# Two tiles by one DMA in the merge stage of a streaming encoder step

## The chip, the cores and the metric

One core of one Trainium2 chip runs the whole program. The metric is device time in microseconds of one execution; three executions of the kernel before were timed, and one more was taken with the hardware profiler. All tensors are float32. Matrix products are done as three products of split operands (high x high, high x low, low x high), which is why many tiles have an "h" and an "l" part.

## The reference

One layer for 2048 new frames and 64 frames of a running stream, model width 1024:

```python
def layer_inputs(x, norm_g, w_in, b_gate, qn_g, kn_g):
    h = rmsnorm(x, norm_g) @ w_in                     # 1024 -> 6144 columns
    qa, ka, va, za, qb, kb, vb, zb, ga, gb = jnp.split(h, _split_points(), axis=-1)
    ...
    ga = jax.nn.sigmoid(ga + b_gate[0])               # merge gates, 1024 wide each
    gb = jax.nn.sigmoid(gb + b_gate[1])

def layer_output(x, oa, ob, za, zb, ga, gb, subln_g, lam_init, w_oa, w_ob, w_out):
    oa = (rmsnorm(oa, subln_g) * (1.0 - lam_init)).reshape(B, T, W_A) * jax.nn.silu(za)
    ob = rmsnorm(ob).reshape(B, T, W_B) * jax.nn.silu(zb)
    m = ga * (oa @ w_oa) + gb * (ob @ w_ob)
    return x + m @ w_out
```

oa is the output of differential attention, ob that of multi-scale retention, each 512 wide; attention and retention themselves are not touched by the change.

## The kernel before

The program has three parts that overlap. The input projection (line L554 of the matmuls) makes q, k, v, the gate inputs za and zb and the merge-gate inputs ga and gb, and stores them to DRAM, transposed (channel on the partition, frame along the row). Attention and retention read q, k, v back and store their branch outputs to DRAM as oaT and obT. Then comes the merge, and after it the output projection with the residual.

The merge works on 8 column groups g of GW = 264 frames. For each group and each branch br (0 is attention, 1 is retention), four row tiles kt of 128 channels are loaded: the branch output `on` and its gate's input `z`. `og_fin` does z = silu(z) on ScalarE, on = on x z on POOL, a cast to the high part ogh on ScalarE, and the difference, the low part ogl, on VectorE. For each group there are eight output tiles ct. `m_tile` does 12 matmuls per branch into one PSUM bank (mm for branch 0, s for branch 1): 24 matmuls per tile (L1722, L1723, L1724). The two merge gates gt of the tile are loaded by `gates`, put through tanh on ScalarE by `gate`, multiplied with the two PSUM results on VectorE (L1742), added on POOL (L1746), and stored as mT by `m_fin`. Only then can that gate buffer be loaded again.

The branch weights w_o_diff and w_o_ret are loaded by `load_wo` in pieces of 128x256 (wst) and split into high and low parts (woh and wol, woq). They share the buffers "oz" with on and z. Beside the merge, `b_prep` loads the output weights w_out and splits them and sums of them (bh and bl, bht and blt; L1815, L1818). The output stage `y_group` (L1934) multiplies mT, loaded as a and split as ah and al, with those. VectorE and POOL prepare sums of a (L1756, L1758), and u holds partial results of the output.

ogh and ogl have three sets of four pairs of buffers: two under the tag "og" and one under "ob". One set is in use by each branch of the current group, so the four pairs for branch 1 of the next group find room only when branch 0 of the present group's last tile is done.

What sets the order: the kernel is written out by a list scheduler of its own. Generators (`spawn`, `loop`) advance by priority on a model of the engines' times: `take` waits until a buffer of a tag is free by the model, `give` says from when it is, `ld` and `st` issue DMAs, and P, A, V and G advance the model's TensorE, ScalarE, VectorE and POOL. On the chip each engine then works through its own list in order, and every wait is a real semaphore. All DMAs of the program, loads (L135) and stores (L140), are issued by one queue, SP, in order.

Of the kernel before, what the change touches and what calls it, by code (L numbers as in the profile page):

```python
# [8 lines left out]
F32 = mybir.dt.float32  # L9
# [17 lines left out]
GW = 264  # L27
# [5 lines left out]
BUFS = {"thi": 1, "tlo": 2, "ev": 3, "q": 2, "K": 4, "V": 4, "ath": 2, "atl": 2,  # L33
        "ws": 3, "w": 12, "r_o": 1, "r_sq": 1, "r_y": 1, "r_hi": 1, "r_lo": 1, "state": 2,
        "mm": 2, "s": 2, "at": 2, "pv": 1, "tp": 1,
        "oz": 11, "og": 16, "ob": 8, "gt": 10, "wa": 16, "st": 13, "ac": 16, "u": 9, "xt": 10}
LAT = 250.0
SLACK = 400.0
PACE = 700.0
# [20 lines left out]
class Hybrid:  # L60
# [1545 lines left out]
    def split_fin(self, tag, h, l, s, t, on_pool, slot, key):  # L1606
# [12 lines left out]
        self.give(tag, t)  # L1619
        slot[key] = t  # L1620

    def load_wo(self, br, q):
        csl = slice(256 * (q % 2), 256 * (q % 2) + 256)
        for kt in range(4):
            hl, slot = self.wo[br][kt]
            h, l = hl[q // 2]
            yield from self.take("oz")
            s = self.sb(self.z3p, [128, GW], "oz", "wst")[:, :256]
            t = self.ld(s, self.i[("w_o_diff", "w_o_ret")[br]][0, 128 * kt:128 * kt + 128, 256 * q:256 * q + 256],
                        1 << 17)  # L1630
            self.spawn(self.split_fin("oz", h[:, csl], l[:, csl], s, t, (kt + q) % 3 == 0, slot, q), 2)
            yield self.pe

    def out_prep(self):
        pa = self.z3p
        self.wo = [[([[self.sb(self.zq, [128, 512], "wa", "woq", F32R) for n in "hl"],
                      [pa.tile([128, 512], F32R, tag=f"wo{n}{br}{kt}", name=f"wo{n}{br}{kt}") for n in "hl"]], {})
                    for kt in range(4)] for br in range(2)]
        for br in range(2):
            yield from self.load_wo(br, 0)  # L1640
        for g in range(8):
            gsl = slice(GW * g, GW * g + GW)
            for br, (oT, zT) in enumerate(((self.oaT, self.zaT), (self.obT, self.zbT))):
                for kt in range(4):
                    yield from self.take("oz", 2)
                    on = self.sb(pa, [128, GW], "oz", "on")
                    z = self.sb(pa, [128, GW], "oz", "z")
                    self.ld(z, zT[kt][:, gsl], 1 << 17)
                    t = self.ld(on, oT[kt][:, gsl], 1 << 17)
                    og = []  # L1650
                    self.ogs.append(og)
                    self.spawn(self.og_fin(on, z, t, og, (2 * g + br) % 3 == 2), 1)
                    yield self.pe
            if g == 0:
                self.spawn(self.gates(), 0)
                for q in range(1, 4):
                    for br in range(2):
                        yield from self.load_wo(br, q)
                yield lambda: self.b_left < 13

    def og_fin(self, on, z, t, og, third):
        nc = self.nc
        yield t
        nc.scalar.activation(z, z, AF.Silu)
# [12 lines left out]
        nc.scalar.copy(h, on)  # L1677
        t = self.A(GW, t)
        yield t
        nc.vector.tensor_sub(l, on, h.bitcast(F32))  # L1680
        t = self.V(GW + 80, t)
        self.give("oz", t)
        og.append((h, l, t))

    def gates(self):
        for n in range(64):
            g, ct = divmod(n, 8)
            yield from self.take("gt", 2)
            pair = [self.sb(self.z3p, [128, GW], "gt") for _ in range(2)]
            for gt, gT in zip(pair, (self.gaT, self.gbT)):  # L1690
                t = self.ld(gt, gT[ct][:, GW * g:GW * g + GW], 1 << 17)
            self.spawn(self.gate(n, ct, pair, t), 0)
            yield self.pe

    def gate(self, n, ct, pair, t):
# [39 lines left out]
    def m_fin(self, g, ct, pss):  # L1735
        nc = self.nc
        yield lambda: 8 * g + ct in self.gts
        gs, tg = self.gts.pop(8 * g + ct)
        for br in range(2):
            ps, tag, t = pss[br]  # L1740
            yield max(t, tg)
            nc.vector.scalar_tensor_tensor(out=gs[br], in0=gs[br], scalar=1.0, in1=ps, op0=ALU.add, op1=ALU.mult)  # L1742
# [553 lines left out]
```

## Time and profile before

| | us |
|---|---|
| median of 3 runs | 1947.14 (1945.34 to 1948.15) |
| the profiled execution | 1945.82 |
| its span, first to last instruction | 1944.0 |
| TensorE busy | 1927.5 |
| VectorE, ScalarE, POOL busy | 1166.6, 964.9, 490.1 |
| merge, first to last matmul start | 1574.9 to 1772.9 |
| output stage from | 1773.0 |

In rows of the profile, PE is TensorE, DVE is VectorE, ACT is ScalarE and SPq is SP's queue; "out<-in" names the tiles an instruction writes and reads; what stands in brackets at the end of a timeline row is how long the engine stood idle before it, and the instruction that ended this. A timeline row "x4" merges four instructions. The mean granted clock of TensorE over the span is 0.998 of full speed.

### The profile page before, as it was taken

The numbers are of one execution on the slowest core, as the hardware profiler recorded it, in microseconds if no ns is written. First come the engines' busy times: TensorE is split into PE (matmuls) and PEld (weight loads), VectorE is DVE, ScalarE is ACT, GpSimd is POOL, SyncE is SP. The second block draws the span as 40 slices with busy tenths as digits, with TensorE's granted clock in tenths as the row PEclk, the third lists the DMA queues.
The fourth block names the chain that finished last, engine by engine and source line by source line (L and its number), as shares of the span: only waits on it lengthen the run. The fifth ranks groups of instructions, "written<-read, shape, count | busy, mean of one in ns | idle before, by whom it ended". The sixth has DMA issues, their size and how long they took to land.

```text
span 1944.0 us, 33842 instructions
## 1 busy us (share of the span) xinstructions
PE 1927.5 (99%) x11984; PEld 1731.2 (89%) x11984; DVE 1166.6 (60%) x2798; ACT 964.9 (50%) x2072; POOL 490.1 (25%) x429
## 2 busy tenths in 40 slices
PE   9999999999999999999999999999999999999999
PEld 8779999999988899999998888888888889998887
DVE  6753777646666336648856757845773376545643
ACT  7443766544434235535765646544563445653321
POOL 4310112112122121211121111112113356543422
PEclk9999999999999999999999999999999999999999
DMA  7747454335566655654344253363133678866651
GB/s 235 240 151 199 143 143 132 106 102 156 163 192 187 166 148 168 202 183 141 112 120 128 76 146 96 99 185 116 63 99 108 190 229 259 264 196 189 190 151 65
DMA packets 372074, 303.32 MB, mean 156 GB/s; under 512 B 77440, under 2 KB 334720, under 8 KB 371904
## 3 DMA queue, kind: packets, MB, share of 16 engines
q1 hardware_dynamic: 371904, 301.16, 52.6%
q8 instruction: 94, 1.54, 0.4%
q14 instruction: 76, 0.62, 0.1%
HBM read 195.87 MB, written 100.14 MB: 152 GB/s over the span
## 4 chain that ended last, share of the span: by engine, by line
PE 88%; DVE 5%; DMA 3%; POOL 1%; issue 1%; ACT 1%; SPq 1%; DVEq 0%; POOLq 0%; ACTq 0%
PE mm L554 51%; PE mm L1934 4%; PE s L1052 3%; PE s L1053 3%; PE at L1160 3%; PE at L1934 2%; PE pv L1139 2%; PE pv L1140 2%; PE pv L1138 2%; PE s L1934 1%; PE s L1723 1%; PE s L1724 1%; PE pv L1521 1%; PE mm L1723 1%; PE s L1722 1%
## 5 line engine op out<-in xcount | busy, mean ns | idle before, releaser
L514 POOL TENSOR_TENSOR wl<-ws,wh 128x512 fp32r<-128x512 f32 x191 | 261.4, 1380 | 896.2 <-ACT wh L504 544.9
L554 PE MATMUL mm<-xh,wh 128*128 128x512 f32 (+2 forms) x1280 | 460.7, 360 | 0.0
L554 PE MATMUL mm<-xh,wl 128*128 128x512 f32 (+2 forms) x1280 | 452.7, 354 | 0.0
L554 PE MATMUL mm<-xl,wh 128*128 128x512 f32 (+2 forms) x1280 | 451.9, 353 | 0.0
L554 PEld LDWEIGHTS mm<-xh,wl 128*128 128x128 f32 x1280 | 241.0, 188 | 31.7
L554 PEld LDWEIGHTS mm<-xh,wh 128*128 128x128 f32 x1280 | 241.4, 189 | 29.1 <-issue 0.2
L554 PEld LDWEIGHTS mm<-xl,wh 128*128 128x128 f32 x1280 | 241.6, 189 | 27.8
L554 PE MATMUL mm<-wh,xh 128*128 128x256 f32 (+1 forms) x768 | 236.7, 308 | 0.0
L554 PE MATMUL mm<-wh,xl 128*128 128x256 f32 (+1 forms) x768 | 231.3, 301 | 0.0
L554 PE MATMUL mm<-wl,xh 128*128 128x256 f32 (+1 forms) x768 | 231.0, 301 | 0.0
L1175 DVE TENSOR_TENSOR atl<-at,ath 128x512 fp32r<-128x512 f32 (+1 forms) x144 | 93.7, 659 | 136.2 <-ACT ath L1173 136.1
L504 ACT CAST wh<-ws 128x512 fp32r<-128x512 f32 x192 | 117.0, 617 | 112.6 <-PE mm L554 90.3
L1091 ACT ACTIVATE row<-row,a_mx 128x1024 f32<-128x1024 f32 (+7 forms) x160 | 153.7, 962 | 24.5 <-DVE a_mx L1071 24.3
L554 PEld LDWEIGHTS mm<-wh,xh 128*128 128x128 f32 x768 | 146.3, 190 | 7.1 <-issue 0.5
L554 PEld LDWEIGHTS mm<-wl,xh 128*128 128x128 f32 x768 | 146.4, 191 | 6.7 <-issue 0.5
L554 PEld LDWEIGHTS mm<-wh,xl 128*128 128x128 f32 x768 | 146.3, 190 | 5.5
L865 DVE TENSOR_TENSOR ev<-mm,rsb 128x512 f32<-128x512 f32 x140 | 83.0, 593 | 112.8 <-PE mm L554 112.4
L1173 ACT CAST ath<-at 128x512 fp32r<-128x512 f32 (+1 forms) x144 | 78.7, 563 | 141.5 <-PE at L1160 138.4
L1061 DVE CUSTOM_DVE_ANT_0 row<-s,dfar 128x512 f32<-128x512 f32 (+2 forms) x192 | 118.2, 630 | 46.4 <-PE s L1053 45.9
L1052 PE MATMUL s<-K,q 128*128 128x512 f32 (+3 forms) x320 | 118.4, 374 | 0.7 <-DVE a_acc L1061 0.7
L1053 PE MATMUL s<-K,q 128*128 128x512 f32 (+3 forms) x320 | 115.2, 362 | 0.0
L1110 ACT ACTIVATE row<-row,a_w 128x1024 f32<-128x1024 f32 (+4 forms) x96 | 85.1, 898 | 34.4 <-DVE a_w L1105 31.2
(342 smaller groups left out, 4193.5 us busy)
## 6 DMA issues: line engine op xcount, KB each, us to landing
ws<-in_w_in_dram SPq DMA_DIRECT2D x192, 256.0 KB, 3.1
q<-qT SPq DMA_DIRECT2D x128, 128.0 KB, 3.0
V<-vN SPq DMA_DIRECT2D x24, 512.0 KB, 5.4
K<-kT SPq DMA_DIRECT2D x48, 256.0 KB, 4.3
a<-mT SPq DMA_DIRECT2D x34, 256.0 KB, 4.1
gt<-gaT SPq DMA_DIRECT2D x64, 132.0 KB, 3.2
gt<-gbT SPq DMA_DIRECT2D x64, 132.0 KB, 3.1
mT<-gt SPq DMA_DIRECT2D x64, 132.0 KB, 3.0
```

The lines of the kernel that those rows point to most:

```text
L504: self.nc.scalar.copy(h, st)
L514: self.nc.gpsimd.tensor_sub(l, st, h.bitcast(F32))
L554: nc.tensor.matmul(ps, p, q, start=c == 0 and i == 0, stop=c == KC - 1 and i == 2)
L865: nc.vector.tensor_mul(ev, ps, rsb)
L1052: nc.tensor.matmul(ps, q1s, kk, start=True, stop=False)
L1053: nc.tensor.matmul(ps, q2s, kk, start=False, stop=True)
L1061: nc.vector.tensor_tensor_reduce(out=units[k0 // 1024][:, k0 % 1024:k0 % 1024 + n], in0=ps, in1=tab, scale=-SLOPES[h], scalar=3.0e38, op0= ...
L1091: nc.scalar.activation(u, u, AF.Exp, bias=mx, scale=-1.0, accum_out=lp[:, k:k + 1])
L1110: nc.scalar.activation(u1, u1, AF.Identity, scale=w[:, 1:2])
L1173: nc.scalar.copy(ah[:, :w], at[:, :w])
L1175: nc.vector.tensor_sub(al[:, :w], at[:, :w], ah[:, :w].bitcast(F32))
L1934: nc.tensor.matmul(q[b], u, v, start=fresh and c == 0 and m == 0, stop=c == 3 and m == 2, skip_group_check=True)
```

## The change

Each branch output and its gate's input get one DRAM tensor ozT with the two side by side for each partition, and the two merge gates one tensor gT. The stores write to views of them. One DMA then loads on and z as one tile of 128x2x264, one DMA loads both merge gates of a tile, and one DMA loads two pieces of a branch's weights. The buffers change from 11 single tiles to 5 double ones under "oz", and from 10 single to 5 double under "gt". Arithmetic instructions stay the same in number and size. A double buffer is given back once, when both halves are done: z's half no longer returns after POOL's product, and gt's second half no longer after POOL's sum.

```diff
-        "oz": 11, "og": 16, "ob": 8, "gt": 10, "wa": 16, ...
+        "oz": 5, "og": 16, "ob": 8, "gt": 5, "wa": 16, ...
 ...
-        self.zaT = tc.dram_tile([4, 128, 8 * GW], F32, name="zaT")
-        self.zbT = tc.dram_tile([4, 128, 8 * GW], F32, name="zbT")
-        self.gaT = tc.dram_tile([8, 128, 8 * GW], F32, name="gaT")
-        self.gbT = tc.dram_tile([8, 128, 8 * GW], F32, name="gbT")
-        self.oaT = tc.dram_tile([4, 128, 8 * GW], F32, name="oaT")
-        self.obT = tc.dram_tile([4, 128, 8 * GW], F32, name="obT")
+        self.ozT = [tc.dram_tile([4, 128, 2, 8 * GW], F32, name=f"ozT{br}") for br in range(2)]
+        self.gT = tc.dram_tile([8, 128, 2, 8 * GW], F32, name="gT")
 ...
     def load_wo(self, br, q):
-        for kt in range(4):
+        for k2 in range(2):
             yield from self.take("oz")
-            s = self.sb(self.z3p, [128, GW], "oz", "wst")[:, :256]
-            t = self.ld(s, self.i[("w_o_diff", "w_o_ret")[br]][0, 128 * kt:128 * kt + 128, 256 * q:256 * q + 256],
-                        1 << 17)
-            self.spawn(self.split_fin("oz", h[:, csl], l[:, csl], s, t, (kt + q) % 3 == 0, slot, q), 2)
+            s = self.sb(self.z3p, [128, 2, GW], "oz", "wst")[:, :, :256]
+            t = self.ld(s, self.i[("w_o_diff", "w_o_ret")[br]][0, 256 * k2:256 * k2 + 256, 256 * q:256 * q + 256]
+                        .rearrange("(c p) n -> p c n", p=128), 1 << 18)
+            box = []
+            for u in range(2):
+                kt = 2 * k2 + u
+                ...
+                self.spawn(self.split_fin("oz", h[:, csl], l[:, csl], s[:, u], t, (kt + q) % 3 == 0, slot, q, box), 2)
 ...
     def out_prep(self):
-                    yield from self.take("oz", 2)
-                    on = self.sb(pa, [128, GW], "oz", "on")
-                    z = self.sb(pa, [128, GW], "oz", "z")
-                    self.ld(z, zT[kt][:, gsl], 1 << 17)
-                    t = self.ld(on, oT[kt][:, gsl], 1 << 17)
+                    yield from self.take("oz")
+                    both = self.sb(pa, [128, 2, GW], "oz", "oz")
+                    t = self.ld(both, self.ozT[br][kt][:, :, gsl], 1 << 18)
 ...
     def og_fin(self, on, z, t, og, third):
         nc.gpsimd.tensor_mul(on, on, z)
         t = self.G(GW, t)
-        self.give("oz", t)
 ...
     def gates(self):
-            yield from self.take("gt", 2)
-            pair = [self.sb(self.z3p, [128, GW], "gt") for _ in range(2)]
-            for gt, gT in zip(pair, (self.gaT, self.gbT)):
-                t = self.ld(gt, gT[ct][:, GW * g:GW * g + GW], 1 << 17)
+            yield from self.take("gt")
+            both = self.sb(self.z3p, [128, 2, GW], "gt")
+            t = self.ld(both, self.gT[ct][:, :, GW * g:GW * g + GW], 1 << 18)
 ...
     def m_fin(self, g, ct, pss):
         nc.gpsimd.tensor_add(gs[0], gs[0], gs[1])
         t = self.G(GW, t)
-        self.give("gt", t)
```

SP issues 1408 DMAs in place of 1552. TensorE's list is the same instruction by instruction. The lists of ScalarE, VectorE and POOL hold the same instructions and are the same up to the merge's first loads; from there on the scheduler puts them in another order.

ScalarE at the passage from column group 1 to group 2, the splits for branch 1 of group 2 (ogh) being the last in each list shown. Before:

```order
L1664 ACTIVATE z<-z 128x264
L1698 ACTIVATE gt<-gt,bg 128x264 x2
L1664 ACTIVATE z<-z 128x264
L1815 CAST bht_18301<-wst 128x512
L1815 CAST bht_18299<-wst 128x512
L1698 ACTIVATE gt<-gt,bg 128x264 x2
L1815 CAST bht_18303<-wst 128x512
L1677 CAST ogh<-on 128x264 x8
```

Now (the line numbers are those of the changed file, and z is a half of oz):

```order
L1698 ACTIVATE gt<-gt,bg 128x264 x6
L1666 ACTIVATE oz<-oz 128x264
L1814 CAST bht_18240<-wst 128x512
L1814 CAST bht_18238<-wst 128x512
L1678 CAST ogh<-oz 128x264 x4
L1814 CAST bht_18242<-wst 128x512
L1698 ACTIVATE gt<-gt,bg 128x264 x2
```

The first four ogh stand ahead of the third bht and of a pair of gt, and the next group's four follow later, one at a time.

VectorE at the same passage, with the low parts ogl. Before:

```order
L1742 SCALAR_TENSOR_TENSOR gt<-gt,mm 128x264
L1742 SCALAR_TENSOR_TENSOR gt<-gt,s 128x264
L1818 TENSOR_TENSOR blt_18302<-wst,bht_18301 128x512
L1818 TENSOR_TENSOR blt_18300<-wst,bht_18299 128x512
L1742 SCALAR_TENSOR_TENSOR gt<-gt,mm 128x264
L1742 SCALAR_TENSOR_TENSOR gt<-gt,s 128x264
L1818 TENSOR_TENSOR blt_18304<-wst,bht_18303 128x512
L1680 TENSOR_TENSOR ogl<-on,ogh 128x264 x8
```

Now:

```order
L1817 TENSOR_TENSOR blt_18241<-wst,bht_18240 128x512
L1817 TENSOR_TENSOR blt_18239<-wst,bht_18238 128x512
L1681 TENSOR_TENSOR ogl<-oz,ogh 128x264 x3
L1742 SCALAR_TENSOR_TENSOR gt<-gt,mm 128x264
L1742 SCALAR_TENSOR_TENSOR gt<-gt,s 128x264
L1681 TENSOR_TENSOR ogl<-oz,ogh 128x264
L1817 TENSOR_TENSOR blt_18243<-wst,bht_18242 128x512
```

Three of the four ogl for branch 1 moved ahead of the pair of gate products, and all four ahead of the third blt.

VectorE at the start of the output stage, after the last gate product. Before:

```order
L1742 SCALAR_TENSOR_TENSOR gt<-gt,s 128x264
L1758 TENSOR_TENSOR a<-a 128x512 x2
L1860 TENSOR_TENSOR al<-a,ah 128x512
L1984 TENSOR_TENSOR u<-s,u 128x512
L1860 TENSOR_TENSOR al<-a,ah 128x512 x4
```

Now:

```order
L1742 SCALAR_TENSOR_TENSOR gt<-gt,s 128x264
L1757 TENSOR_TENSOR a<-a 128x512 x2
L1859 TENSOR_TENSOR al<-a,ah 128x512 x3
L1983 TENSOR_TENSOR u<-s,u 128x512
L1859 TENSOR_TENSOR al<-a,ah 128x512 x2
```

Two al moved ahead of the u that reads what POOL adds. On POOL, the first two sums of a moved ahead of the first u there:

```order
L1746 TENSOR_TENSOR gt<-gt 128x264 x15
L1756 TENSOR_TENSOR u<-u,oxt 128x512
L1756 TENSOR_TENSOR a<-a 128x512 x2
L1756 TENSOR_TENSOR u<-u,oxt 128x512 x2
```

```order
L1746 TENSOR_TENSOR gt<-gt 128x264 x12
L1755 TENSOR_TENSOR a<-a 128x512 x2
L1755 TENSOR_TENSOR u<-u,oxt 128x512 x3
```

The first fence is POOL's list before, the second its list now.

More of the change, by code (lines that the diff above doesn't have):

```diff
@@ L35 @@
         "mm": 2, "s": 2, "at": 2, "pv": 1, "tp": 1,
-        "oz": 11, "og": 16, "ob": 8, "gt": 10, "wa": 16, "st": 13, "ac": 16, "u": 9, "xt": 10}
+        "oz": 5, "og": 16, "ob": 8, "gt": 5, "wa": 16, "st": 13, "ac": 16, "u": 9, "xt": 10}
 LAT = 250.0
@@ L160, in scratch @@
         self.kbT = tc.dram_tile([4, 128, TT], F32, name="kbT")
-        self.zaT = tc.dram_tile([4, 128, 8 * GW], F32, name="zaT")
-        self.zbT = tc.dram_tile([4, 128, 8 * GW], F32, name="zbT")
-        self.gaT = tc.dram_tile([8, 128, 8 * GW], F32, name="gaT")
-        self.gbT = tc.dram_tile([8, 128, 8 * GW], F32, name="gbT")
-        self.oaT = tc.dram_tile([4, 128, 8 * GW], F32, name="oaT")
-        self.obT = tc.dram_tile([4, 128, 8 * GW], F32, name="obT")
+        self.ozT = [tc.dram_tile([4, 128, 2, 8 * GW], F32, name=f"ozT{br}") for br in range(2)]
+        self.gT = tc.dram_tile([8, 128, 2, 8 * GW], F32, name="gT")
+        (self.oaT, self.zaT), (self.obT, self.zbT) = ([[t[h][:, k] for h in range(4)] for k in range(2)]
+                                                      for t in self.ozT)
+        self.gaT, self.gbT = ([self.gT[c][:, k] for c in range(8)] for k in range(2))
         self.mT = tc.dram_tile([8, 128, 8 * GW], F32, name="mT")
@@ L1604, in ret_sample, with split_fin @@
         self.state, self.t_state = None, 0.0
-    def split_fin(self, tag, h, l, s, t, on_pool, slot, key):
+    def split_fin(self, tag, h, l, s, t, on_pool, slot, key, box):
         nc = self.nc
@@ L1618, in split_fin @@
             t = self.V(n + 120, t)
-        self.give(tag, t)
+        box.append(t)
+        if len(box) == 2:
+            self.give(tag, max(box))
         slot[key] = t
@@ L1623, in load_wo @@
         csl = slice(256 * (q % 2), 256 * (q % 2) + 256)
-        for kt in range(4):
-            hl, slot = self.wo[br][kt]
-            h, l = hl[q // 2]
+        for k2 in range(2):
             yield from self.take("oz")
-            s = self.sb(self.z3p, [128, GW], "oz", "wst")[:, :256]
-            t = self.ld(s, self.i[("w_o_diff", "w_o_ret")[br]][0, 128 * kt:128 * kt + 128, 256 * q:256 * q + 256],
-                        1 << 17)
-            self.spawn(self.split_fin("oz", h[:, csl], l[:, csl], s, t, (kt + q) % 3 == 0, slot, q), 2)
+            s = self.sb(self.z3p, [128, 2, GW], "oz", "wst")[:, :, :256]
[4 more added lines that the diff above has]
+                kt = 2 * k2 + u
+                hl, slot = self.wo[br][kt]
+                h, l = hl[q // 2]
+                self.spawn(self.split_fin("oz", h[:, csl], l[:, csl], s[:, u], t, (kt + q) % 3 == 0, slot, q, box), 2)
             yield self.pe
@@ L1642, in out_prep @@
             gsl = slice(GW * g, GW * g + GW)
-            for br, (oT, zT) in enumerate(((self.oaT, self.zaT), (self.obT, self.zbT))):
+            for br in range(2):
                 for kt in range(4):
-                    yield from self.take("oz", 2)
-                    on = self.sb(pa, [128, GW], "oz", "on")
-                    z = self.sb(pa, [128, GW], "oz", "z")
-                    self.ld(z, zT[kt][:, gsl], 1 << 17)
-                    t = self.ld(on, oT[kt][:, gsl], 1 << 17)
+                    yield from self.take("oz")
+                    both = self.sb(pa, [128, 2, GW], "oz", "oz")
+                    t = self.ld(both, self.ozT[br][kt][:, :, gsl], 1 << 18)
                     og = []
                     self.ogs.append(og)
-                    self.spawn(self.og_fin(on, z, t, og, (2 * g + br) % 3 == 2), 1)
+                    self.spawn(self.og_fin(both[:, 0], both[:, 1], t, og, (2 * g + br) % 3 == 2), 1)
                     yield self.pe
@@ L1687, in gates @@
             g, ct = divmod(n, 8)
-            yield from self.take("gt", 2)
-            pair = [self.sb(self.z3p, [128, GW], "gt") for _ in range(2)]
-            for gt, gT in zip(pair, (self.gaT, self.gbT)):
-                t = self.ld(gt, gT[ct][:, GW * g:GW * g + GW], 1 << 17)
-            self.spawn(self.gate(n, ct, pair, t), 0)
+            yield from self.take("gt")
+            both = self.sb(self.z3p, [128, 2, GW], "gt")
+            t = self.ld(both, self.gT[ct][:, :, GW * g:GW * g + GW], 1 << 18)
+            self.spawn(self.gate(n, ct, [both[:, br] for br in range(2)], t), 0)
             yield self.pe
```

## The prediction

> **What bounds the kernel now.** I read the page's head first, then busy time by stage, then TensorE's own rows.
>
> ```profile
> span 1944.0 us, 33842 instructions
> PE 1927.5 (99%) x11984; PEld 1731.2 (89%) x11984; DVE 1166.6 (60%) x2798; ACT 964.9 (50%) x2072; POOL 490.1 (25%) x429
> ```
>
> TensorE is busy 99% of the span, so only its idle or slowed time can be won. The stages, with the granted clock and the DMA engines' busy share at the end of each row:
>
> ```profile
> core 0: us, PE busy (x) PEld busy (x) DVE busy (x) ACT busy (x) POOL busy (x), PEclk, DMA share, GB/s
> 1524.00:1575.00 51.00, 51.00 (x229) 42.22 (x227) 22.01 (x37) 27.61 (x67) 23.61 (x26) 1.00 0.80 248
> 1575.00:1599.00 24.00, 23.21 (x189) 22.83 (x188) 18.93 (x29) 12.20 (x31) 15.82 (x17) 1.00 0.66 203
> 1623.00:1650.00 27.00, 24.22 (x174) 23.81 (x173) 18.97 (x34) 16.66 (x41) 16.13 (x17) 0.87 0.82 251
> 1773.00:1944.00 171.00, 165.59 (x714) 132.27 (x712) 83.84 (x111) 44.68 (x80) 57.41 (x41) 1.00 0.50 149
> ```
>
> The changed loads are issued from about 1530 us on. Up to 1575 us TensorE has no gap, and ahead of the merge the change gives every engine the same instructions in the same order, so nothing can move there but the DRAM addresses that some stores go to. The merge (L1722 to L1724) follows. TensorE's timeline shows its first matmul, the break near 1626 us, the start of the second tile of the last column group, and the first matmul of the output stage (L1934):
>
> ```profile
> 1574.90 0.29 PE L1722 MATMUL mm<-ogh,woq 128*128 128x264 f32 x1
> 1624.69 0.28 PE L1724 MATMUL mm<-ogh,woq 128*128 128x264 f32 x1
> 1626.05 0.39 PE L1722 MATMUL s<-ogh,woq 128*128 128x264 f32 x1 [1.08 <-ACT ogh L1677]
> 1628.14 0.59 PE L1723 MATMUL s<-ogl,woq 128*128 128x264 f32 x1 [1.70 <-DVE ogl L1680]
> 1752.56 0.28 PE L1722 MATMUL mm<-ogh,woq 128*128 128x264 f32 x1
> 1773.03 0.40 PE L1934 MATMUL mm<-bh,ah 128*128 128x512 f32 x1
> ```
>
> 64 tiles take 1773.03 - 1574.90 = 198.1 us. The last 7, undisturbed, take 20.47 us, or 2.924 each; 64 at that pace are 187.2. So the merge loses 10.9 us. More than half of that is one place, the passage from column group 1 to group 2. There TensorE waits 1.08 us for a high part of the gated branch output (ScalarE, L1677) and 1.70 us for its low part (VectorE, L1680), and then runs at half clock. In narrow stretches (us, PE busy, clock, DMA share, GB/s):
>
> ```profile
> 1628.00:1630.00 2.00, 1.86 (x8) 0.50 0.82 252
> 1630.00:1632.00 2.00, 2.00 (x11) 0.50 0.77 236
> 1632.00:1634.00 2.00, 2.00 (x11) 0.50 0.84 257
> 1634.00:1636.00 2.00, 2.00 (x18) 0.96 0.75 240
> 1780.00:1790.00 10.00, 8.19 (x35) 1.00 0.98 313
> ```
>
> Six us at half clock and 2 us at 0.96 lose 3.0 + 0.08 = 3.1 us. With the idle time, 2.78 us, the passage costs 5.9 us. The last row belongs to the start of the output stage: 1.8 us idle within 10, with no loss of clock. Hence 1.8 us of waiting close together leaves the clock alone, and 2.78 us halves it.
>
> The Trainium skill, "TensorE: Matmul & The Clock Gate", What's actually happening, has the clock fall to half after at least one idle window of about 3.4 us. Neither wait here is that long, and the clock fell all the same, so the trace is stricter than the page. By the page alone the slow stretch would not be charged to these waits, and the sum below would be 3.1 us smaller.
>
> **Why TensorE waited there.** ScalarE's and VectorE's rows around it:
>
> ```profile
> 1622.90 0.42 ACT L1664 ACTIVATE z<-z 128x264 f32<-128x264 f32 x1 [1.32 <-DMA z<-zaT]
> 1623.23 1.12 ACT L1815 CAST bht<-wst 128x512 fp32r<-128x512 f32 x2
> 1624.26 0.92 ACT L1698 ACTIVATE gt<-gt,bg 128x264 f32<-128x264 f32 x2
> 1625.08 0.60 ACT L1815 CAST bht<-wst 128x512 fp32r<-128x512 f32 x1
> 1625.59 2.60 ACT L1677 CAST ogh<-on 128x264 fp32r<-128x264 f32 x8
> 1623.87 2.05 DVE L1818 TENSOR_TENSOR blt<-wst,bht 128x512 fp32r<-128x512 f32 x2 [2.75 <-ACT bht L1815]
> 1625.84 0.41 DVE L1742 SCALAR_TENSOR_TENSOR gt<-gt,mm 128x264 f32<-128x264 f32 x1
> 1626.52 0.68 DVE L1818 TENSOR_TENSOR blt<-wst,bht 128x512 fp32r<-128x512 f32 x1
> 1627.12 2.57 DVE L1680 TENSOR_TENSOR ogl<-on,ogh 128x264 fp32r<-128x264 f32 x4
> ```
>
> Both engines work in order. ScalarE lost 1.32 us to a late gate input (z). Behind it stood three casts of output weights (bht) and two tanh of merge gates (gt) before the urgent splits. VectorE idled 2.75 us for bht, then did two blt, a pair of gate products and a third blt before the first ogl. So two things made the splits late: a load, and the work placed ahead of them.
>
> **The loads.** The late z and the next DMA on SP's queue:
>
> ```profile
> 1618.63 0.38 SPq L135 DMA_DIRECT2D z<-zaT  x1
> 1619.11 0.39 SPq L135 DMA_DIRECT2D on<-oaT  x1
> ```
>
> SP issues one DMA each 0.48 us (1618.63 to 1619.11), and every load and store passes through this one queue. The z was used at 1622.90, 4.3 us after its issue.
>
> **The change, part by part.**
>
> *Fewer issues.* 64 loads of z and on, 64 of gates and 16 of branch weights go: 144 x 0.48 = 69 us of SP's queue over some 230 us. None of that is on TensorE's path by itself; SP's lag reaches TensorE only where a load is late on ScalarE, as at 1622.90. Bytes and row lengths stay, so the DMA engines, busy 0.82 of the worst stretch, are not relieved.
>
> The Trainium skill, "DMA: Bandwidth & Descriptors", Issuing engines are not separate DMA queues, says that a sequencer's time to start a DMA is usually small beside the DMA. That speaks against this change; one DMA at a time the trace agrees (0.48 against 3.2 us to land, below). If it held for the whole queue, this part would bring nothing, and rival A would be the result.
>
> *The new order at the passage.* On ScalarE the four urgent ogh now stand behind two bht casts. The pair of gt (0.92) and the third bht (0.60) fall behind them, so ogh comes about 1.5 us sooner and the wait of 1.08 us goes. On VectorE three ogl stand directly behind two blt; the gate products and the third blt go behind them, so the first ogl starts where the gate product stood, at 1625.84 in place of 1627.12: 1.28 us sooner. 2.78 - 1.28 = 1.5 us of idle time would be left if the loads were as late as before, less than the 1.8 that left the clock alone. That gains 1.28 + 3.1 = 4.4. If the load's 1.32 us goes too, nearly all 5.9 does. I take 5.0, with 0 and 5.9 as ends.
>
> *The buffers.* Of a pair of halves, one used to come free after POOL's product, and now both do after ogl. The nearest row is what SP already waited for that:
>
> ```profile
> SPq L135 <- DVE ogl L1680: 2.8, 9, 0.5
> ```
>
> At most 0.5 us at a time. It bites where the lead is shortest, at the passage from group 0 to group 1, where the next group's loads have to follow the splits. I take a loss of 0.5, from 0 to 2.
>
> *Longer landings.* These rows give KB and median us to land:
>
> ```profile
> gt<-gaT SPq DMA_DIRECT2D x64, 132.0 KB, 3.2
> a<-mT SPq DMA_DIRECT2D x34, 256.0 KB, 4.1
> ```
>
> Two loads of 132 KB are both there 0.48 + 3.2 = 3.7 us after the first issue; one of 264 KB, by the row of 256 KB, in some 4.1, 0.4 us later. For the gates this is covered:
>
> ```profile
> SPq L135 <- DMA mT<-gt: 14.5, 14, 1.9
> 1754.45 1.05 SPq L140 DMA_DIRECT2D mT<-gt  x1
> 1757.29 0.32 SPq L135 DMA_DIRECT2D gt<-gbT  x1
> ```
>
> SP's loads wait for merge stores to land before the change too (first row: 14.5 us in 14 waits). This load, the second of its pair, was issued 2.84 us after the store five tiles back, about when that had landed, so a pair's issue is no later than now. By the 3.2 us above it lands at 1760.5. Its tile is the sixth of the last group, whose first half ends at 1752.56 + 4.5 x 2.924 = 1765.7, so some 4 us are left for two tanh. Cost 0, at the outside 1. The branch weights are loaded ahead of 1575, under the stretch without a gap: 0.
>
> *The start of the output stage.* VectorE's and POOL's order shifts here too.
>
> ```profile
> 1782.98 0.50 PE L1934 MATMUL at<-bht,al 128*128 128x512 f32 x1 [1.07 <-DVE al L1860]
> 1786.30 0.50 PE L1934 MATMUL mm<-bht,ah 128*128 128x512 f32 x1 [0.74 <-ACT u L1962]
> 1781.18 0.69 DVE L1984 TENSOR_TENSOR u<-s,u 128x512 f32<-128x512 f32 x1 [2.49 <-POOL u L1756]
> 1779.85 1.29 POOL L1756 TENSOR_TENSOR u<-u,oxt 128x512 f32<-128x512 f32 x1 [4.97 <-DMA oxt<-in_x_prompt_dram]
> 1781.10 2.96 POOL L1756 TENSOR_TENSOR a<-a 128x512 f32<-128x512 f32 x2
> ```
>
> The awaited al stood on VectorE behind a u that waited for POOL, which waited 4.97 us for a load. Now three al stand ahead of that u, and POOL does its two sums (a) before it waits for the load. That frees the 1.07, and likely the 0.74, whose u stood on ScalarE behind casts of those sums. I take 1.5, from 0 to 1.8.
>
> *Sum:* 5.0 + 1.5 - 0.5 = 6.0 us. The profiled execution took 1945.82 us (span 1944.0), so it becomes 1939.8. That execution is 1.3 us below the median, 1947.14; the forecast against the median is **1941.1 us**.
>
> **Rivals.**
>
> A, *no change*: the DMA engines, not SP's issues, make the loads late. The passage then waits as before and trips the clock, and only the output stage gains: 1.5 - 0.5 = 1.0, or 1946.1 us. For it: a DMA share of 0.82 and 4.3 us to land with SP only a slot behind. Against it: the splits come sooner in the order even with equal loads.
>
> B, *slower*: keeping both halves until ogl makes the group's loads late at the passage from 0 to 1 (about 1600 us), and the clock trips there while the old trip also stays. It decides from a wait of some 2.3 us, between the 1.8 and 2.78 above; its price is that wait and 3.1 us, 5.4 in all. With no other gain than the 1.0 of A the time is 1947.1 - 1.0 + 5.4 = 1951.5. Against it: between two passages there are 23 us (8 x 2.924) in which to load the next eight pairs.
>
> C, *more*: with SP ahead, the smaller waits go too. All 10.9 + 1.8, less the 0.8 us idle in group 0 (1575 to 1599 above: 24.00 - 23.21), where VectorE's order hardly changes: 11.9, or 1935.2.
>
> **How the numbers follow.** Chances: forecast 0.50, A 0.22, B 0.14, C 0.14. The forecast's own range is 1939.4 to 1944.7 (passage 5.9 or 4.4, output stage 1.8 or 0, buffers 0 or 2). The range 1935.0 to 1949.5 takes in C and A and leaves out most of B and a little below C. About 0.2%, 3.9 us, is what a measurement here can tell from no change. C and nearly all of the forecast lie beyond it (0.03 of its 0.50 within): faster 0.61. With A, no change is 0.25. B gives slower: 0.14.
>
> **What would show it.** Right: the wait for ogl near 1626 us is under 1.8 us and the clock stays at 1.00 through the merge; 64 tiles take about 193 us; the two waits after 1780 us are gone; SP issues 144 fewer. Wrong: a clock below 1.00 anywhere in the merge, waits for ogl over 2 us at any passage, or silu rows on ScalarE that wait longer for the pairs than for z before.

## The result, and the profile after

The changed kernel takes 1965.1 us (median of 6 runs, 1962.4 to 1974.2), the kernel before 1946.8 beside it: a ratio of 1.0103, 95% interval 1.0080 to 1.0126, worked out from the single runs and not from the medians. One of the six runs of the kernel before took 6745.8 us and is left out of the ratio. It is slower by 18.3 us, where a gain of 6.0 was forecast. The profiled execution took 1964.23 us. The head of its page:

```profile
span 1962.5 us, 33732 instructions
PE 1934.1 (99%) x11984; PEld 1734.9 (88%) x11984; DVE 1166.6 (59%) x2798; ACT 963.2 (49%) x2072; POOL 486.7 (25%) x429
```

The engines do the same work. TensorE's busy time grew by 6.6 us (1934.1 against 1927.5), part of it work at half clock; the rest of the span's growth is idle time. The place is the merge. TensorE's timeline has the first matmul of the merge, which stood at 1574.90 before, and the first of the output stage, which stood at 1773.03:

```profile
1577.13 0.29 PE L1722 MATMUL mm<-ogh,woq 128*128 128x264 f32 x1
...
1793.33 0.39 PE L1933 MATMUL mm<-bh,ah 128*128 128x512 f32 x1
```

The merge ends 20.3 us later. From there to the end of the span it takes 169.2 us, where it took 171.0: the output stage is 1.8 us shorter. So the span's growth of 18.5 us is 20.3 lost up to the end of the merge, less 1.8 gained behind it. The merge itself took 216.2 us in place of 198.1, 18.1 more. The other 2.2 lie ahead of it and are taken for scatter between executions: in the fourteen profiles of this document the merge starts between 1574.55 and 1577.13, and at 1574.55 in the kernel with the gate given back later, whose work on the four engines is in the same order up to there.

What TensorE waited for in the changed merge (1575 to 1794 us; us in total, times, longest), and the same stretches by clock as in the prediction (the clock is third from the end):

```profile
PE mm L1722 <- DVE gt L1742: 8.0, 5, 2.7
PE s L1722 <- ACT ogh L1678: 5.4, 4, 2.7
PE s L1723 <- DVE ogl L1681: 3.7, 9, 1.2
```

```profile
1623.00:1650.00 27.00, 21.92 (x174) 21.09 (x174) 14.92 (x28) 15.49 (x37) 13.12 (x15) 1.00 0.76 234
1650.00:1676.00 26.00, 23.29 (x162) 22.49 (x161) 15.07 (x31) 12.83 (x32) 11.26 (x13) 0.87 0.68 204
1749.00:1776.00 27.00, 22.87 (x154) 21.82 (x154) 9.73 (x22) 11.73 (x30) 9.12 (x13) 0.87 0.54 156
```

17.1 us of waiting, and a lower clock in two stretches. The place that the forecast rested on, the passage to group 2 near 1626 us, keeps its clock; it falls at the passage to group 3 near 1658 us instead, and twice around group 6, from 1754 and from 1771 us (the last section has the rows). The largest group of waits is for gt: VectorE's gate products are late, so the PSUM banks of "mm" are not given back in time.

The chain of SP is behind it. Its waits for merge stores in the merge, before and after (us, times, longest):

```profile
SPq L135 <- DMA mT<-gt: 20.4, 19, 1.9
```

```profile
SPq L135 <- DMA mT<-gt: 76.1, 42, 4.2
```

SP's timeline around the start of the last group of the changed kernel shows why (start, duration):

```profile
1764.99 0.55 SPq L140 DMA_DIRECT2D mT<-gt  x1
1768.26 0.52 SPq L135 DMA_DIRECT2D gt<-gT  x1
1768.84 0.59 SPq L140 DMA_DIRECT2D mT<-gt  x1
1772.23 0.52 SPq L135 DMA_DIRECT2D gt<-gT  x1
1772.80 0.96 SPq L140 DMA_DIRECT2D mT<-gt  x1
1775.78 0.52 SPq L135 DMA_DIRECT2D gt<-gT  x1
1776.40 0.56 SPq L140 DMA_DIRECT2D mT<-gt  x1
```

A store goes out; the next gate load waits some 3.3 us until it has landed; the next store stands behind that load in SP's list and goes out some 0.6 us after it. One turn takes 3.80 us on average ((1776.40 - 1764.99) / 3), and TensorE needs 2.924 for a tile. What came of it on ScalarE and TensorE:

```profile
1763.30 0.92 ACT L1698 ACTIVATE gt<-gt,bg 128x264 f32<-128x264 f32 x2 [2.85 <-DMA gt<-gT]
1766.86 0.92 ACT L1698 ACTIVATE gt<-gt,bg 128x264 f32<-128x264 f32 x2 [2.63 <-issue]
1767.69 1.34 ACT L1678 CAST ogh<-oz 128x264 fp32r<-128x264 f32 x4
```

```profile
1768.13 0.39 PE L1722 MATMUL s<-ogh,woq 128*128 128x264 f32 x1 [0.70 <-ACT ogh L1678]
```

ScalarE stands before the tanh because the gate is late (the trace names the load for the first wait, and nothing for the second), and the urgent splits (ogh) of the next group stand behind the tanh. So the late gates also make the passages between groups late.

### The profile page after: what moved, and what is told of

It reads as the page before. It is cut to its first block, busy times and chain, and to the rows that moved or that the text cites. A ratio compares the mean times of both kernels' runs of the same rounds, so it can differ in the third digit from the quotient of the medians.

```text
span 1962.5 us, 33732 instructions
## 1 busy us (share of the span) xinstructions
PE 1934.1 (99%) x11984; PEld 1734.9 (88%) x11984; DVE 1166.6 (59%) x2798; ACT 963.2 (49%) x2072; POOL 486.7 (25%) x429
## 4 chain that ended last, share of the span: by engine, by line
PE 83%; DMA 7%; DVE 5%; ACT 2%; issue 1%; SPq 1%; POOL 1%; DVEq 0%; ACTq 0%; POOLq 0%
PE mm L553 49%; PE mm L1933 4%; PE s L1051 3%; PE s L1052 3%; PE at L1159 3%; PE at L1933 2%; DMA mT<-gt 2%; DMA oz<-ozT 2%; PE pv L1138 2%; PE pv L1139 2%; PE pv L1137 2%; PE s L1933 1%; PE pv L1520 1%; PE tp L733 1%; PE pv L1404 1%
```

## The experiments

Each kernel was timed beside the kernel before, 4 to 11 executions each. Differences below are between medians of one set (the kernel before took 1946.79 us beside the change, and 1946.67, 1946.24 and 1946.05 in the three sets of experiments); ratios have their 95% interval.

| | us | ratio to before | difference |
|---|---|---|---|
| the change | 1965.09 | 1.0103 (1.0080 to 1.0126) | +18.3 |
| gates in pairs only | 1962.99 | 1.0089 (1.0075 to 1.0102) | +16.3 |
| branch outputs in pairs only | 1947.61 | 1.0009 (1.0000 to 1.0018) | +0.9 |
| change, sum in a tile of its own | 1942.56 | 0.9980 (0.9971 to 0.9989) | -4.1 |
| the same, second timing | 1943.44 | 0.9988 (0.9979 to 0.9997) | -2.6 |
| change, gate given back later in the plan | 1968.56 | 1.0120 (1.0104 to 1.0135) | +21.9 |
| change, 6 gate pairs, 4 branch pairs | 1974.38 | 1.0147 (1.0133 to 1.0161) | +28.1 |
| change, gate pair by two loads | 1951.43 | 1.0027 (1.0017 to 1.0037) | +5.2 |
| change, stores issued by POOL | 1949.35 | 1.0014 (1.0005 to 1.0023) | +3.1 |
| no pairs, sum tiles | 1950.31 | 1.0026 (1.0018 to 1.0035) | +4.1 |
| gates in pairs, sum tiles | 1946.10 | 1.0000 (0.9991 to 1.0009) | 0.0 |
| branch outputs in pairs, sum tiles | 1942.49 | 0.9982 (0.9973 to 0.9990) | -3.6 |
| both in pairs, sum tiles, stores by POOL | 1950.16 | 1.0025 (1.0016 to 1.0034) | +4.1 |

**Which part is it?** The two halves of the change alone. In the first, oz and the weights stay single:

```diff
-            yield from self.take("gt", 2)
-            pair = [self.sb(self.z3p, [128, GW], "gt") for _ in range(2)]
-            for gt, gT in zip(pair, (self.gaT, self.gbT)):
-                t = self.ld(gt, gT[ct][:, GW * g:GW * g + GW], 1 << 17)
+            yield from self.take("gt")
+            both = self.sb(self.z3p, [128, 2, GW], "gt")
+            t = self.ld(both, self.gT[ct][:, :, GW * g:GW * g + GW], 1 << 18)
```

> Only the merge gates lie in pairs (five tiles of two halves); branch outputs and their weights are loaded one by one as before. Theory Q (queue): a gate pair comes free only when its sum's store has landed, the load that takes it stands in SP's queue directly behind that store, and the next store stands behind the load, so SP goes once per tile at store, landing (3.4 us), load, 3.75 us in all against TensorE's 2.92. Then this kernel is slow like the changed one: 1958 to 1968 us, and SP's loads wait 60 us or more for merge stores. Theory O (the branch pairs, held until ogl, are late): about as before, 1942 to 1949. Theory L (a load of 264 KB lands later, whoever frees it): slow too, some 1955 to 1965, but with SP's waits for merge stores near the 20 us of before.

In the second this part is left as before and the rest of the change is made.

> Only the branch outputs with their SiLU inputs, and the branch weights, lie in pairs; merge gates are loaded one by one as before. Theory Q: not slow; 1940 to 1948 us, with SP's waits for merge stores near the 20 us of before. Theory O: slow, 1955 to 1967. Theory L: between the two, 1948 to 1957, for the pairs' landing (4.5 us) is the longer one.

Measured: 1963.0 and 1947.6. The gates carry 16.3 of the 18.3 us. In that kernel SP's loads wait 58.7 us for merge stores, near the 60 of theory Q and far from the 20 of theory L. The order of the work is not the cause there: in the traces TensorE's and VectorE's lists are those of the kernel before, instruction by instruction (by operation and tile name), and two instructions of ScalarE and one of POOL have moved. Theory O, the prediction's rival B in another form, is out: with branch pairs alone the time can hardly be told from no change. Their passage to group 2 shows no wait at all; in their whole merge TensorE waits 0.5 us for ogl. But it waits 8.9 us for gt, and SP's loads wait 41.8 us for merge stores, twice what they did before. Their small difference is a net of two: the merge takes 202.0 us in place of 198.1, the part behind it 168.8 in place of 171.0.

**Is it the wait for the store?** POOL writes its sum to a small tile; the pair is given back before the store:

```diff
+        yield from self.take("ms")
+        ms = self.sb(self.z3p, [128, GW], "ms")
-        nc.gpsimd.tensor_add(gs[0], gs[0], gs[1])
+        nc.gpsimd.tensor_add(ms, gs[0], gs[1])
         t = self.G(GW, t)
+        self.give("gt", t)
         yield t
-        t = self.st(self.mT[ct][:, GW * g:GW * g + GW], gs[0], 1 << 17)
-        self.give("gt", t)
+        t = self.st(self.mT[ct][:, GW * g:GW * g + GW], ms, 1 << 17)
+        self.give("ms", t)
```

> The whole change, but POOL writes its sum to a small tile of its own (three of them, four gate pairs in place of five), and the pair is given back after the sum, ahead of the store. Theory Q: no load waits for a store any more; 1940 to 1950 us, although there is a pair less. Theory K (only capacity: with five pairs a load comes late because too few are in flight): slower than the changed kernel or equal, 1960 to 1975, as there is one pair fewer, unless the store's 3.4 us outweighs it. Theories O and L: still slow, 1955 to 1967, since branch pairs and sizes are those of the change.

Measured: 1942.6, faster than before, with a pair less. No load waits for a store in the merge, the clock stays at 1.00 there, and the first matmul of the output stage is 7.2 us earlier than before the change:

```profile
1765.87 0.39 PE L1936 MATMUL mm<-bh,ah 128*128 128x512 f32 x1
```

The loads are as large as in the change and land even later. Median us to land, changed kernel first, then this one:

```profile
gt<-gT SPq DMA_DIRECT2D x64, 264.0 KB, 3.5
```

```profile
gt<-gT SPq DMA_DIRECT2D x64, 264.0 KB, 4.1
```

So a later landing of the gates themselves, theory L as I had put it, is not the cause.

**Does it help to put the load further back?** One number:

```diff
-        self.give("gt", t)
+        self.give("gt", t + 2500)
```

> The whole change, with one number altered: the planner is told that a store gives its gate pair back 2.5 us later. Nothing is computed otherwise; the gate load only moves back in SP's order, to stand behind a later store than the one that frees it. Theory Q: SP no longer stops right behind each store, so the time falls by 8 to 20 us against the changed kernel, to 1945 to 1957. Theory K (capacity): loads come later still, 1965 to 1975. Theories O and L: no change beyond 4 us, 1961 to 1969.

Measured: 1968.6, nominally what theory K says, but the expectation rested on a wrong idea of the code. The plan fixes the order of TensorE, ScalarE, VectorE and POOL (`manual_schedule(engines=MANUAL(ET))`); SP is not among them, and each load still stood behind the store that frees its tile, as 82.3 us of waits for stores in 44 waits show. It says nothing about Q.

**More tiles?** `"oz": 4, "gt": 6` in place of 5 and 5, so that the memory stays the same.

> The whole change with six gate pairs in place of five, paid for with one of the five branch pairs. Each gate load still stands in SP's queue directly behind the store that frees its tile. Theory Q (SP's queue, in order, stops at store, landing, load once per tile): one more tile does not shorten that cycle, 1958 to 1970 us. Theory K (the five tiles are held too long each, some 13 us from load to store and 3.4 to landing, for one tile per 2.92 us): a sixth brings back most of the loss, 1942 to 1952, unless the lost branch pair costs as much.

Measured: 1974.4, above the ranges of both theories. The sixth pair recovers nothing, and SP's waits for stores stay (82.7 us in 45). That speaks for Q against K; how much of the extra 9.8 us is the lost branch pair was not separated.

**Holding or size?** The pair stays one tile, held until the store has landed, but comes by two loads:

```diff
-            t = self.ld(both, self.gT[ct][:, :, GW * g:GW * g + GW], 1 << 18)
+            for k in range(2):
+                t = self.ld(both[:, k], self.gT[ct][:, k, GW * g:GW * g + GW], 1 << 17)
```

> The whole change, but each gate pair is filled by two loads of 132 KB, so only the holding of both halves until the store has landed is left of the gates' part. Theories Q and K (the holding): as slow as the changed kernel or slower, 1962 to 1972 us. Theory L (the larger load's later landing): most of the loss is gone, 1943 to 1955.

Measured: 1951.4, in the range of L and outside that of Q and K. So holding, with 64 more issues than the change and with the change's gains elsewhere, leaves 5.2 of the 18.3 us, and the size of the load brings the other 13.1. The order of the work is the same: the lists of TensorE, ScalarE, VectorE and POOL are those of the change, instruction by instruction; SP's own list differs by more than the split loads, in where some loads stand. Yet the kernel with the small tile has the same large loads and is fast. Both facts agree when the landing of the stores is looked at. In calm stretches near the end of the merge (before; the change; this kernel; the kernel with the small tile), min, median and max us from a store's issue to its landing:

```profile
L140 SPq DMA_DIRECT2D mT<-gt x7: 383/384/1049, 1739.0 to 1754.5; - x7
DMA to landing us min/median/max: 2.0/2.1/2.8
```

```profile
L140 SPq DMA_DIRECT2D mT<-gt x6: 557/592/962, 1768.8 to 1787.6; - x6
DMA to landing us min/median/max: 2.9/3.1/3.3
```

```profile
L140 SPq DMA_DIRECT2D mT<-gt x6: 377/386/1030, 1756.6 to 1770.9; - x6
DMA to landing us min/median/max: 2.1/2.1/2.4
```

```profile
L140 SPq DMA_DIRECT2D mT<-ms x6: 591/598/1155, 1738.8 to 1753.5; - x6
DMA to landing us min/median/max: 3.0/3.2/4.6
```

A store of the same 132 KB lands in 2.1 us when the load issued just ahead of it is of 132 KB, and in 3.1 when it is of 264 KB, though the DMA engines were less busy there (a share of 0.39 in 1767 to 1788 us of the change, 0.55 in 1738 to 1755 before). Over all 64 stores, many of them behind other loads, the difference is smaller: the medians are 3.0 us before and 3.4 in the change, and directly behind a gate load 2.8 (31 stores) and 3.2 (30).

The load at 1768.26 landed at 1771.77, and the store of 1768.84 at 1772.18, just behind it; the next load went out at 1772.23. So it is in all twelve kernels here whose stores SP issues: of 503 stores directly behind a gate load none landed ahead of that load, and the median of each kernel is 0.41 to 0.43 us behind it. With small tiles the longer landing is there as well, but no load waits for it. I call this theory QL: the wait for the store is in the loop, and the larger load makes that wait longer, which makes one turn 3.80 us long, past TensorE's 2.92. Before, seven stores near the end of the merge, the first and the last of them below, made six turns of 2.58 us each:

```profile
1736.44 0.42 SPq L140 DMA_DIRECT2D mT<-gt  x1
...
1751.90 0.38 SPq L140 DMA_DIRECT2D mT<-gt  x1
```

The Trainium skill, "DMA: Bandwidth & Descriptors", Queues, rings and completion order, says that a DMA's semaphore increment lands only after every earlier write of that DMA engine. By that rule a store cannot be seen as landed before the load issued ahead of it on the same engines; the 503 landings agree.

**Is it the queue?** The same large loads, held as long, but the next store no longer stands behind a waiting load:

```diff
-        t = self.st(self.mT[ct][:, GW * g:GW * g + GW], gs[0], 1 << 17)
+        nc.gpsimd.dma_start(self.mT[ct][:, GW * g:GW * g + GW], gs[0])
+        t = self.pe + (1 << 17) / 150.0 + DMA_LAT
```

> The whole change, but the 64 merge stores are issued by POOL, right behind its sum, and not by SP. A gate load still waits for the store to land, but no store stands behind a waiting load. Theory Q: 1942 to 1953 us. Theory K: the residence is as long as before, 1958 to 1970. POOL's own cost to issue a store is not known from the traces; if it is near a microsecond, POOL (some 16 us busy in 24) has room for it.

Measured: 1949.3, as Q said. The lists of TensorE, ScalarE, VectorE and, but for its stores, POOL are again those of the change, and 12 of SP's 1344 loads and other stores have moved. SP's loads wait for stores more than ever, and it costs little:

```profile
SPq L135 <- DMA mT<-gt: 106.8, 46, 7.6
```

So it is mostly not the waiting load that made the change slow, but the stores behind it. This kernel does not leave the landing quite alone: its stores' median is 3.1 us, the change's 3.4. Together the last two kernels open the loop at two places, one at the length of the landing, one at the queue, and each takes away most of the loss.

**Is the early release the gain, or the pairs?** A square of four kernels with small sum tiles and the same memory: nothing in pairs, gates, branch outputs with their weights, both.

> Not the change at all: the kernel before, loads one by one, with POOL's sum in a small tile of its own (three of them, eight gate halves in place of ten, ten branch halves in place of eleven), so that a gate half comes free after the sum. It stands against the kernel with pairs and small tiles, 1942.6 us. If pairing brings that gain (fewer issues on SP): this one is as before or slower, 1945 to 1955. If the early release brings it and pairing nothing: 1939 to 1944.

> Corner of the square: gates in four pairs, branch outputs single (ten halves), small sum tiles. Theory QL (a load that waits for a store's landing, with the next store behind it, cost the changed kernel its time, and a larger load ahead of the store made that landing longer; with the wait gone, fewer issues on SP help): better than the 1950.3 with nothing in pairs, 1943 to 1949 us. Rival: the gates' pairs gain nothing even when released early, and the branch pairs bring all of it: 1948 to 1953.

> Corner of the square: branch outputs in five pairs, gates single (eight halves), small sum tiles. Theory QL: between the corners, 1943 to 1949 us. Rival as above (the branch pairs bring all): 1940 to 1945, the same as with both.

> The kernel with both pairings and the small tile for POOL's sum once more, beside the three below on one chip: 1940 to 1945 us, as before at 1942.6. It is the corner of a square of four (branch outputs in pairs or single, gates in pairs or single, always with three small sum tiles and the same bytes of on-chip memory); the opposite corner, nothing in pairs, took 1950.3.

Measured: 1950.3, 1946.1, 1942.5 and 1943.4 (1942.6 the first time). Early release alone, with two gate halves and a branch half given up for the small tiles, makes the kernel before slower by 4.1 us. Branch pairs bring 7.8 where gates are single and 2.7 to 3.5 where they are in pairs. Gate pairs bring 4.2 where branch outputs are single and nothing where they are in pairs. The rival (branch pairs bring all) holds for the best corner, QL's in-between holds for the gates' corner; neither had both. The best version has only branch outputs and weights in pairs and the sum in a small tile, level with that of both pairs: 0.9982 of the time before (0.9973 to 0.9990).

**Still fewer issues on SP?** The kernel with both pairs and small tiles, its stores issued by POOL.

> Both pairings, small sum tiles, and POOL issues the 64 merge stores. With the small tiles no load of SP waits for a store, but SP's loads waited 48.8 us for POOL's sum. Theory QL: no more to win from the stores' place, 1940 to 1946 us. Rival: SP's queue is still what sets the pace, and 64 issues fewer on it give 2 us or more: 1937 to 1940.

Measured: 1950.2; both theories missed by 4 us or more. POOL's rows show what was left out: a store takes 0.58 us of POOL, mostly after 0.4 of waiting for its own sum (40 of 64), so a tile costs POOL about 1 us more, and its sums come later. SP's loads wait 91.3 us for them, where they waited 50.5 in the second timing of the kernel whose stores SP issues. That is read from the profile and was not tested by itself.

**Why the best versions gain only 4 us of 7.** The merge with both pairs and small tiles ends 7.2 us earlier, but the output stage is then not ready. Its wait in TensorE's timeline of that kernel, and the stretches around it (the first number after the times is TensorE's busy time, the clock is third from the end):

```profile
1775.61 0.80 PE L1936 MATMUL mm<-bht,al 128*128 128x512 f32 x1 [3.62 <-DVE al L1862]
```

```profile
1770.00:1775.00 5.00, 1.99 (x9) 1.32 (x7) 1.18 (x2) 1.26 (x3) 2.47 (x3) 0.90 0.78 221
1775.00:1780.00 5.00, 4.39 (x10) 3.47 (x11) 4.13 (x5) 1.66 (x3) 1.69 (x2) 0.50 1.02 350
1780.00:1785.00 5.00, 5.00 (x21) 4.02 (x20) 0.00 (x0) 2.18 (x4) 2.22 (x2) 0.92 1.07 313
```

One wait of 3.62 us, and 2.6 us lost behind it to a half clock that sets in during the wait and lasts to about 1781 (half of 4.39 and 0.08 of 5.00). The part from the first matmul of the output stage takes 174.9 us in place of 171.0: 3.9 of the 7.2 are given back. Removing that wait was not tried.

## Why the prediction was wrong, and what of it was right

*Fewer issues.* The 144 are gone (64 loads of gates and 64 of branch pairs are left of 256, 16 of weights of 32), and no gain of theirs shows in the changed kernel. The square shows that branch pairs are worth 3 to 8 us once no load waits for a store; whether that is SP's queue or the planner's other order was not separated. The Trainium skill's rule that the time to start a DMA is small beside the DMA (cited in the prediction, "DMA: Bandwidth & Descriptors", Issuing engines are not separate DMA queues) is not refuted: 64 issues moved from SP to POOL, at POOL's own price, gained nothing.

*The new order at the passage to group 2* helped the way the step said. TensorE's rows there:

```profile
1627.25 0.39 PE L1722 MATMUL s<-ogh,woq 128*128 128x264 f32 x1 [0.86 <-ACT ogh L1678]
1628.84 0.39 PE L1723 MATMUL s<-ogl,woq 128*128 128x264 f32 x1 [1.20 <-DVE ogl L1681]
1630.55 0.39 PE L1723 MATMUL s<-ogl,woq 128*128 128x264 f32 x1 [0.35 <-DVE ogl L1681]
```

2.41 us of waits in place of 2.78 and no loss of clock: a gain of 0.4 + 3.1 = 3.5, where I took 5.0. The size was off; that the late gates had reached this place too is likely, for with branch pairs alone the waits are gone, but was not tested by itself. That the clock held was luck: 2.41 us is above the 1.8 that the prediction knew to be safe, and the last section shows that it hung on where the waits fell.

*The start of the output stage* gained 1.8 us (171.0 to 169.2) where I took 1.5, and one wait of 0.2 us is left of two of 1.07 and 0.74.

*The buffers.* For branch pairs the 0.5 us was fair: SP's longest wait for ogl is 0.5 us in the change too. But only they were priced. The gates' halves are held longer as well, and that was passed over: before, the first load of a pair needed only POOL's sum, and only the second waited for the store. This term measured 5.2 us (the kernel with two loads, as a net with the gains of the rest) where it had been given nothing.

*Longer landings* is the step that failed: "a pair's issue is no later than now", cost 0, at the outside 1. It measured 13 us. The load's own landing was not what was mis-sized: I took 4.1 us, and it was 3.5. I set one load's issue against one store's landing, 2.84 us, found 4 us to spare before the tile was needed, and kept the store's landing fixed. But store, landing, load and next store are one loop in an in-order queue. A margin of 4 us says nothing of a loop that loses 0.9 us each tile where nothing else delays it; its turn had to be set against TensorE's 2.924, and the landing in it depends on the load ahead of the store. The row was at hand: SP already waited for stores 14 times in its own list.

*Rival B* had the sign and part of the mechanism (halves held longer, loads late, the clock trips) on the wrong buffers and at the wrong place: the passage from group 0 to group 1 (near 1600 us) has no such wait. Its 1951.5 us was 13.6 too low. My own marks of a wrong forecast, a clock below 1.00 in the merge, showed.

## What to carry to other kernels

Where loads and stores share one in-order queue and a load waits for a store to land, work out the turn of that loop (store, landing, load, next store) and set it against the consumer's pace; slack for one load is no answer. Before two tiles are joined in one transfer, ask when each of them came free and which came free without a store: a joined buffer is as late as its later half. A result that is to be stored may be better put in a tile of its own than in a buffer that the next load waits for: with pairs it was worth 22 us here, but in the kernel before, where other buffers were given up for it, it lost 4.

## What was not expected of the hardware

The landing of a store is not its own: in calm stretches 2.1 us behind a load of 132 KB, 3.1 behind one of 264 KB. And the sum of idle time close together, by which the prediction set a line between 1.8 and 2.78 us, does not decide when the clock halves. At the passage to group 2 in the changed kernel 0.86, 1.20 and 0.35 us, 2.41 within 4.2, left it at 1.00. One wait of 2.71 us halved it at the passage to group 3, and at the passage to group 7 three waits of 0.70 (shown above), 0.39 and 0.26, 1.35 within 3.2, did so too. A wait of 2.67 us left it alone, and one of 2.65 halved it. TensorE's timeline has the waits:

```profile
1642.45 0.39 PE L1722 MATMUL mm<-ogh,woh 128*128 128x264 f32 x1 [2.67 <-DVE gt L1742]
...
1658.63 0.59 PE L1722 MATMUL s<-ogh,woq 128*128 128x264 f32 x1 [2.71 <-ACT ogh L1678]
...
1752.49 0.39 PE L1722 MATMUL mm<-ogh,woh 128*128 128x264 f32 x1 [2.65 <-DVE gt L1742]
...
1769.68 0.39 PE L1723 MATMUL s<-ogl,woq 128*128 128x264 f32 x1 [0.39 <-DVE ogl L1681]
1770.58 0.40 PE L1723 MATMUL s<-ogl,woq 128*128 128x264 f32 x1 [0.26 <-DVE ogl L1681]
```

The Trainium skill, "TensorE: Matmul & The Clock Gate", What's actually happening, has a window of about 3.4 us that runs freely. The traces agree: in the changed kernel the clock changes at 1658.37, 1665.19, 1753.94, 1757.35, 1771.01 and 1774.42 us, and the later ones lie 2, 28, 29, 33 and 34 times 3.413 us behind the first. The time can thus be cut into windows of 3.41 us. Seven of them hold most of the waits above; three are followed by a window at half clock, shown with them (the first number in a row's brackets counts TensorE's matmuls, the clock is third from the end):

```profile
1627.65:1631.06 3.41, 1.87 (x13) 1.66 (x14) 3.41 (x8) 2.75 (x7) 1.07 (x2) 1.00 0.96 322
1637.89:1641.30 3.41, 1.89 (x16) 1.68 (x14) 0.91 (x2) 2.04 (x6) 3.33 (x5) 1.00 0.95 316
1654.96:1658.37 3.41, 0.97 (x8) 0.75 (x7) 0.00 (x0) 1.01 (x3) 0.00 (x0) 1.00 0.43 119
1658.37:1661.78 3.41, 3.15 (x11) 2.74 (x12) 3.11 (x8) 2.11 (x7) 0.82 (x1) 0.50 0.76 198
...
1685.68:1689.09 3.41, 2.04 (x14) 1.74 (x14) 2.79 (x8) 3.25 (x9) 0.74 (x1) 1.00 0.78 220
1723.22:1726.63 3.41, 1.81 (x14) 1.82 (x15) 2.70 (x7) 2.49 (x7) 2.99 (x5) 1.00 0.44 126
1750.53:1753.94 3.41, 1.45 (x12) 1.45 (x12) 3.00 (x7) 3.10 (x8) 2.00 (x4) 1.00 0.61 154
1753.94:1757.35 3.41, 3.41 (x18) 3.41 (x17) 0.69 (x2) 0.00 (x0) 0.51 (x1) 0.50 0.87 245
...
1767.60:1771.01 3.41, 2.09 (x10) 1.47 (x11) 2.84 (x7) 2.25 (x7) 0.82 (x1) 1.00 0.37 85
1771.01:1774.42 3.41, 3.41 (x18) 3.41 (x17) 0.63 (x2) 0.92 (x2) 0.76 (x1) 0.50 0.34 95
```

A window without waits holds 30 or 31 matmuls. After 8, 10 and 12 the clock halved; after 13 to 16 it did not. In the other thirteen traces too every change lies on such a grid. Their merges and this one have 792 whole windows at full clock: it halved after each of the 20 with at most 11 matmuls, after none of the 765 with 14 or more, and after 4 of the 7 with 12 or 13. So what counts is how much TensorE does within one window, and a wait counts by where it lies: of the 2.67 us 1.52 lie in one window and 1.15 in the next, of the 2.65 us 1.96 lie in one. That is read from the traces; no kernel was made to test it.
